# A hybrid encoder layer on one core: the last refill moves into the first output block, the descending norm comes one lane step later, and the two lanes get other rates

## The chip, the core and the metric

The kernel runs on one core of one Trainium2 chip. The core has a matrix engine (TensorE, PE in the profile, with PEld for its weight loads), a vector engine (VectorE, DVE), an activation engine (ScalarE, ACT), a general engine (GpSimd, POOL) and a queue engine (SyncE, SP) that issues nearly all transfers here. Operands lie in SBUF, matrix products are gathered in banks of PSUM. The metric is the device time of one execution in microseconds.

## The reference

One layer of an encoder with three groups of heads side by side, in 32-bit floats: `x + W_out @ concat[SSD, windowed attention, memory attention](RMSNorm(x))`. The rows are 1024 of a sample and 256 of a prompt, the model width is 2048. Cut to what matters:

```python
hn = rms_norm(x, norm_g)
proj = hn @ w_in
xbc, z_ssd, dt_raw, q, k, v, z_att, mq, z_mem = split_cols(proj, IN_SIZES)
xbc = jax.nn.silu(centred_dwconv(xbc, conv_w, conv_b))
...
y_f = ssd_scan(xs, dt[:, :, 0], A[0], Bm, Cm)
y_b = ssd_scan(xs[:, ::-1], dt[:, ::-1, 1], A[1], Bm[:, ::-1], Cm[:, ::-1])[:, ::-1]
y = (y_f + y_b + d_skip[:, None] * xs).reshape(b, T, SSD_WIDTH)
yg = (y * jax.nn.silu(z_ssd)).reshape(b, T, SSD_GROUPS, SSD_WIDTH // SSD_GROUPS)
o_ssd = rms_norm(yg, ssd_norm_g...)
o_att = window_attention(q, k, v, sink) * jax.nn.silu(z_att)
...
return x + jnp.concatenate([o_ssd, o_att, o_mem], axis=-1) @ w_out
```

`ssd_scan` is a chunked scan with chunks of 128 rows: within a chunk a masked product `C B^T` with decay, between chunks a state that is carried. It is run forwards and backwards over the rows. `ssd_norm_g` is a norm over each of two halves of 512 columns. The memory attention is a softmax attention of every row over 256 memory rows.

## The kernel before, in words

The 1280 rows are ten tiles of 128, in two groups of five. Tiles 0 to 7 are the sample, 8 and 9 the prompt. Group 0 is tiles 0 to 4, group 1 tiles 5 to 9.

**Blocks.** The program is a row of blocks, each a product of the rows of one group with 512 columns (token block, `block_tok`, L258 to L260) or with 256 columns transposed (feature block, `block_feat`, L293 to L295) over 16 places k of the 2048-deep sum. Every 32-bit product is made of three products of rounded parts: weights are split into `wh` and `wl` by `wsplit` (ACT L206, DVE L207), rows into `xH` and `xL`. A k of a token block is 15 products of 128x512, a pair of k's of a feature block 24 products of 128x320. The results gather in five PSUM banks (`acc`) and are taken out at the block's end (`zs`, `qs`, `yt`). Group 0 goes through most of its columns early, in another scheme. The part in question starts at about 540 us; its blocks in order are z1 (group 0), six x blocks, kv, q, za0, za1, z0, z1, mq, zm0, zm1, all of group 1, and then the output blocks o, four token blocks, of group 0's rows through W_out, before the output pair units from about 1575 us.

**Lanes.** All the rest (attention, scan, memory attention) is written as Python generators that hang in two lanes. Lane 0 has the attention (`attn`, `k_prep`), the memory attention (`mem_attn`); lane 1 has `dt_prep`, the ascending scan `ssd_up(t)` for t = 0 to 9 and the descending scan `ssd_down(t)` for t = 7 to 0, then 9 and 8. After each k of a block `pump(rates)` runs as many steps of each lane as `RATES` says: in a token block that number per k, in a feature block per pair of k's. A step is the code between two `yield`s. So where a lane's product stands between block products on PE is set by the rates and by the number of `yield`s; a scheduler then orders the instructions of each engine, moving loads forward. `need(fn, tiles)` runs a lane until the named tiles are done, whatever the rates say. PSUM for lane products is a ring of three banks, shared by all of them: a product waits till the one three before it has been taken out.

**The ascending tile** `ssd_up(t)`: C B^T into `pcb` (L823, L824), its copies `bth`, `btl`, `cb` (L827 to L830), a yield, then `cd`, `cbd`, `dco` on DVE (L833 to L839), and for each half the turned x, `pxs` (L858) with its copy `xs` on DVE (L860), then the decay rows `rf`, `rb` (L850, L922), `fh` and `fl` (L879, L887) and `pst` (L865) for the state.

**The descending tile** `ssd_down(t)`: loads of the part sums `yd`, the gate `zd`, the stored state `st`, and the turned diagonal part `ydT` (L1037); some yields; `norm_ssd`, which multiplies the tile before by its norm factor `yrs` (L998; the factor comes from ACT's sum of squares L1067 and three small POOL instructions, L123, L124, L1078); `diag_in(0)`, which turns `ydT` on PE into `pd` (L1043) and adds it (L1044); a yield; and per half the product with the state `pyb` (L1060), the gate, the sum of squares, a yield, and `turn_ssd(g)`, which turns the finished half of the tile before on PE (`pr`, L1007), copies it out (`so`, L1009) and stores it (`oT`, L1010). Only the tiles that start a descent (7 and 9) have nine yields at the start, the others three.

**The refill.** The output blocks read the rows from four quads of SBUF tiles, places k = 0 to 3, 4 to 7, 8 to 11, 12 to 15: quad 0 from the attention, quad 1 from the memory attention, quads 2 and 3 from the two halves of the scan. They are reloaded from DRAM by `fill_direct`: a load `chd` (L188) at one k, and a lag later a write of `xH` on ACT (L200 with gain, for the scan; L197 without) and of `xL` on DVE (L201, L198). `run` asks `after(q)` at k = 3, 7, 11, 15 of the block ahead, which first makes sure by `need` that the data are finished:

```python
            if after is not None and k % 4 == 3:
                pend.extend(after(k // 4))
```

For the scan that is `need(ssd_down, tiles 0 to 4)` at k = 11 of zm1, the last block ahead of the output blocks. At k = 9 of the third output block all that is left in the lanes is run; then come `seven_load` (L1105, L1106) and the sums for the output pair units, which read the finished rows of group 1.

Of the kernel before, what the change touches and what calls it, by code (L numbers as in the profile page):

```python
# [29 lines left out]
RBB = 4  # L30

RATES = ({'kv': (4.0, 1.0), 'z1': (2.2, 1.7)},
         {'kv': (1.4, 1.5), 'x': (2.1, 2.15), 'q': (2.2, 2.5), 'za': (2.05, 2.5), 'z0': (2.0, 2.6),
          'z1': (1.9, 2.65), 'mq': (1.9, 2.8), 'zm': (1.6, 2.85), 'o': (2.15, 2.25)})
FAR = 1e30

UNITS = (0, 8, 1, 9, 2, 10, 3, 11, 4, 12, 5, 13, 6, 7)
# [7 lines left out]
def hymba_encoder_kernel(  # L45
# [11 lines left out]
    def xrow(t):  # L57
        return x_sample[t * P:(t + 1) * P] if t < NS else x_prompt[(t - NS) * P:(t - NS + 1) * P]
# [24 lines left out]
    def psum(name):  # L83
        return mix.tile([P, 512], F32, tag="mix", name=name)
# [41 lines left out]
    def hv(ap, n=8):  # L126
        return ap.rearrange("p (h d) -> p h d", h=n)
# [50 lines left out]
    pend, loaded = deque(), deque()  # L178
# [31 lines left out]
    def w_laid(src, n):  # L210

        def load(k, raw):
            S.dma_start(raw, src[k])
        return load, n
# [12 lines left out]
    def w_out_rows(c):  # L227
        return w_laid(w_out_laid[c], 512)
# [173 lines left out]
    def ev_out(c0):  # L402
        def f(t, ps):

            if t in (0, 3):
                yt = rp.tile([P, 640], F32, tag="ch", name="yt", bufs=CH)[:, :512]
            else:
                yt = ev.tile([P, 512], F32, tag="evt" if t == 2 else "evu", name="yt")
            S.dma_start(yt, xrow(t)[:, c0:c0 + 512])
            V.tensor_add(yt, ps, yt)  # L410
            S.dma_start(y_first[t * P:(t + 1) * P, c0:c0 + 512], yt)
        return f
# [390 lines left out]
    def wb(name, dtype=F32, shape=(P, 512)):  # L803
        return mp.tile(list(shape), dtype, tag="wb", name=name, bufs=WBB)

    def ssd_up(t):
        first = t in (0, NS)
        last = t in (NS - 1, NT - 1)
        tok = slice(t * P, (t + 1) * P)
# [4 lines left out]
        for g in range(2):  # L814
            x = wb("xc", F32R, shape=(P, 4, P))
# [13 lines left out]
        cb = mp.tile([P, 2, P], F32, tag="cb", name="cb", bufs=1)  # L829
        A.activation(cb, hv(ps[:, :256], 2), AF.Copy)  # L830
        yield
        cd2 = wb("cd2", shape=(P, 2, P))
        V.tensor_mul(cd2, cb, ident.unsqueeze(1).broadcast_to([P, 2, P]))  # L833
        cbd = sm.tile([P, 2], F32, tag="s2", name="cbd", bufs=4)
# [2 lines left out]
        for g in range(2):  # L837
            c = slice(8 * g, 8 * g + 8)
# [31 lines left out]
        for g in range(2):  # L870
            c = slice(g * 512, (g + 1) * 512)
# [121 lines left out]
    def norm_ssd():  # L993

        if "y" in last_y:
            t, ys, rs = last_y.pop("y")
            for g in range(2):
                V.tensor_scalar(out=ys[g], in0=ys[g], scalar1=rs[:, g:g + 1], scalar2=None, op0=ALU.mult)  # L998
                last_y[g] = t, ys[g]
# [12 lines left out]
    def ssd_down(t):  # L1012
        first = t in (0, NS)
        last = t in (NS - 1, NT - 1)
        tok = slice(t * P, (t + 1) * P)
        ss = sm.tile([P, 2], F32, tag="s2", name="yss", bufs=4)
        if not last:
            cc = mp.tile([P, 2, P], F32, tag="btok", name="cc", bufs=1)
            S.dma_start(cc, xbc_d[10:12, :, tok].rearrange("f p c -> p f c"))
        ld = []  # L1020
        for g in range(2):
            c = slice(g * 512, (g + 1) * 512)

            y = mp.tile([P, 512], F32, tag="ya" if t % 2 else "rf", name="yd", bufs=2)
            S.dma_start(y, yp_d[t][:, c])
            if g == 0 and t < 5:
                z = mp.tile([P, 512], F32R, tag="xs", name="zd", bufs=2)
                S.dma_start(hv(z.bitcast(F32), 4), yT_d[:, :, tok])
            else:
                z = mp.tile([P, 512], F32, tag="xs", name="zd", bufs=2)  # L1030
                S.dma_start(z, z_d[g][t])
            st = None
            if not first:
                st = state[:, c] if last else wb("st2")
                S.dma_start(st, sb_d[t][:, c])
            d = mp.tile([P, 4, P], F32R, tag="rb", name="ydT", bufs=RBB)
            S.dma_start(d.bitcast(F32), yd_d[t][:, 4 * g:4 * g + 4, :])  # L1037
            ld.append((y, z, st, d))

        def diag_in(g):  # L1040
            ps = psum("pd")
            for j in range(4):
                T.transpose(ps[:, j * P:(j + 1) * P].bitcast(F32R), ld[g][3][:, j, :], identr)  # L1043
            V.tensor_add(ld[g][0], ld[g][0], ps)  # L1044

        for _ in range(9 if last else 3):
            yield
        norm_ssd()
        diag_in(0)
        yield  # L1050
        for g in range(2):
            c = slice(g * 512, (g + 1) * 512)
            y, z, st, _ = ld[g]
            if g == 0 and t < 5:
                zr, z = z, psum("pz")
                for j in range(4):
                    T.transpose(z[:, j * P:(j + 1) * P].bitcast(F32R), zr[:, j * P:(j + 1) * P], identr)
            if not last:
                pf = psum("pyb")
                T.matmul(pf, cc[:, g, :], state[:, c], start=True, stop=True)  # L1060
                y2 = wb("y3")
                V.tensor_mul(hv(y2), hv(pf), hb(eacs_all[:, t, 16 + 8 * g:24 + 8 * g], 8, 64))
                V.tensor_add(y, y, y2)
            V.tensor_mul(y, y, z)
            if g == 0 and t < 5:
                z = wb("zq")
            A.activation(z, y, AF.Square, scale=0.5, accum_out=ss[:, g:g + 1])  # L1067
            if not first and not last:
                V.tensor_mul(hv(state[:, c]), hv(state[:, c]), hb(cd_all[:, t, 16 + 8 * g:24 + 8 * g], 8, 64))
                V.tensor_add(state[:, c], state[:, c], st)  # L1070
            yield
            turn_ssd(g)
            if g == 0:
                diag_in(1)
                yield
        rs = sm.tile([P, 2], F32, tag="s2", name="yrs", bufs=4)
        rsqrt(rs, ss, 1.0 / 512, 2)
        G.tensor_scalar(out=rs, in0=rs, scalar1=0.5, scalar2=None, op0=ALU.mult)  # L1078
        last_y["y"] = t, [x[0] for x in ld], rs
        yield  # L1080
        if first:
            for _ in range(3):
                yield
            norm_ssd()
            yield
            yield
            for g in range(2):
                turn_ssd(g)
                yield
# [307 lines left out]
    def run(gen, rates, after=None, hold=0, lag=2, extra=None):  # L1397

        for k in gen:
            if after is not None and k % 4 == 3:  # L1400
                pend.extend(after(k // 4))
            if hold:
                for _ in range(2 if k < KT - 4 else 0):
                    if pend:
                        u = pend.popleft()()
                        next(u)
                        next(u)
            else:

                if loaded and (len(loaded) == lag or not pend or k >= KT - 4):  # L1410
                    next(loaded.popleft())
                if pend and k < KT - 4:
                    loaded.append(pend.popleft()())
                    next(loaded[-1])

            if k >= hold:
                pump(rates)
            if extra is not None:
                extra(k)
# [16 lines left out]
        yield  # L1436

    def refill_x(grp):
        def f(q):
            need(x_rows, [grp])  # L1440
            return [part(fill_direct, q, j, x_turned[grp, (4 * q + j) * P:(4 * q + j + 1) * P, :],
                         gain=vec[:, R_G + 4 * q + j:R_G + 4 * q + j + 1], norm=True) for j in range(4)]
        return f

    def refill_o(grp):
        def f(q):
            need((attn, mem_attn, ssd_down, ssd_down)[q], range(grp * 5, grp * 5 + 5))
            return [part(fill_direct, q, j, oT_d[q][grp][:, j, :],
                         gain=None if q < 2 else vec[:, R_SG + 4 * (q - 2) + j:R_SG + 4 * (q - 2) + j + 1])
                    for j in range(4)]  # L1450
        return f
# [63 lines left out]
    def tok(name, w, evac, after=None, grp=0):  # L1515
        run(block_tok(w, 5, evac), RATES[grp][name], after)
# [83 lines left out]
    def gate(name, c, after=None):  # L1600
        for b in range(2):
            feat(name, b, ev_gateT(c, 1, 2 * b), 1, after if b else None)
# [13 lines left out]
    queue(1, ssd_up, range(8, 10))  # L1616
    queue(1, ssd_down, range(9, 7, -1))
    tok("mq", w_in_rows("mq"), ev_raw(mq_d, 5), grp=1)
    gate("zm", 1, refill_o(0))
    queue(0, mem_attn, range(5, 8))  # L1620
    queue(0, mem_swap, [0])
    queue(0, mem_values, [1])
    queue(0, mem_attn, range(8, 10))
    for c in range(2):
        tok("o", w_out_rows(c), ev_out(c * 512), grp=1)
    for c in range(2, 4):
        j0 = 16 * (c - 3)
        for k in block_tok(w_out_rows(c), 5, ev_out(c * 512), before_last=lambda _: beside_step(j0 + 14)):
# [91 lines left out]
```

## Time and profile before

| what | value |
|---|---|
| median of 3 runs | 1795.46 us (1795.38 to 1795.53) |
| profiled execution | 1795.31 us, its span 1793.6 us |
| PE busy | 1777.4 us, 99% of the span, 10838 products |
| DVE, ACT, POOL busy | 1249.9, 919.5, 545.7 us (70%, 51%, 30%) |
| PE's granted clock | 1.00 throughout |
| 560 to 1345 us | PE busy for 775.1 of 785 us |

PE is nearly always busy, and so what it waits for is read from PE's own idle times: a row of the waits names the instruction that came late and what released it, with the total, the number and the longest. A row of the timeline gives start, duration, engine, line, operation, what it writes and reads, and in square brackets the idle time of that engine just before it and the releaser. In the chain of waits a row gives start, duration and what. The rows of the windows give start:end, length, the busy time of PE, PEld, DVE, ACT and POOL (with counts), then the clock, the share of the DMA engines and GB/s.

### The profile page before, as it was taken

What the parts mean: (1) busy time and instruction counts of PE and PEld (TensorE: products, weight loads), DVE (VectorE), ACT (ScalarE), POOL (GpSimd) and SP (SyncE); (2) the same over time, 40 slices, a digit from 0 to 9 for tenths busy, and PEclk for the clock granted to TensorE, in tenths of its full rate; (3) what the DMA queues carried; (4) which work ended last, traced back from release to release, by engine and by line L of the source; (5) the groups of instructions that cost most, each with busy time, mean ns of one, the idle gap of its engine ahead of it and who ended that gap; (6) DMA issues with size and microseconds to landing.
All of it is one profiled execution on the core that took longest, in us unless ns stands there. A gap on an engine that the chain in (4) does not pass through costs nothing. (4 is left out here: it accounts for less than half of the span.)

```text
span 1793.6 us, 31444 instructions
## 1 busy us (share of the span) xinstructions
PE 1777.4 (99%) x10838; PEld 1606.1 (90%) x10838; DVE 1249.9 (70%) x2358; ACT 919.5 (51%) x2049; POOL 545.7 (30%) x900
## 2 busy tenths in 40 slices
PE   9999999999999999999999999999999999999999
PEld 7789999999998989999889977777888888889999
DVE  5595788888768877877665566567775644766665
ACT  6554455554334765756465565544465533433332
POOL 0105889999710100001001000000100000058775
PEclk9999999999999999999999999999999999999999
DMA  8664455445446644343635645557876755644442
GB/s 300 191 179 123 136 153 151 137 149 154 126 152 199 191 141 148 120 161 115 188 111 178 190 147 165 175 154 258 257 225 202 231 181 164 205 145 147 146 142 78
DMA packets 208208, 301.12 MB, mean 168 GB/s; under 512 B 19569, under 2 KB 86193, under 8 KB 208049
## 3 DMA queue, kind: packets, MB, share of 16 engines
q1 hardware_dynamic: 207904, 299.06, 54.4%
q8 instruction: 85, 1.39, 0.3%
q14 instruction: 75, 0.61, 0.1%
q10 hardware_dynamic: 144, 0.06, 0.0%
HBM read 236.36 MB, written 62.69 MB: 167 GB/s over the span
## 5 line engine op out<-in xcount | busy, mean ns | idle before, releaser
L207 DVE TENSOR_TENSOR wl<-wraw,wh 128x512 fp32r<-128x512 f32 (+1 forms) x480 | 347.1, 725 | 232.3 <-ACT wh L206 224.0
L206 ACT ACTIVATE wh<-wraw 128x512 fp32r<-128x512 f32 (+1 forms) x480 | 292.5, 614 | 316.1 <-PE acc L260 154.3
L258 PE MATMUL acc<-wh,xH 128*128 128x512 f32 (+1 forms) x1088 | 419.4, 386 | 0.5 <-DVE v_all L337 0.4
L259 PE MATMUL acc<-wl,xH 128*128 128x512 f32 (+1 forms) x1088 | 410.7, 378 | 0.3 <-DVE wl L207 0.2
L260 PE MATMUL acc<-wh,xL 128*128 128x512 f32 (+1 forms) x1088 | 410.4, 377 | 0.0
L258 PEld LDWEIGHTS acc<-wh,xH 128*128 128x128 f32 x1088 | 204.6, 188 | 38.6 <-issue 3.8
L259 PEld LDWEIGHTS acc<-wl,xH 128*128 128x128 f32 x1088 | 204.8, 188 | 38.4 <-DVE wl L207 2.7
L260 PEld LDWEIGHTS acc<-wh,xL 128*128 128x128 f32 x1088 | 204.4, 188 | 36.8 <-issue 0.2
L293 PE MATMUL acc<-xH,wh 128*128 128x320 f32 x640 | 202.6, 317 | 0.0
L206 ACT ACTIVATE sh<-ws 128x384 fp32r<-128x384 f32 x176 | 91.4, 523 | 214.8 <-POOL ws L1205 123.0
L294 PE MATMUL acc<-xL,wh 128*128 128x320 f32 x640 | 198.9, 311 | 0.0
L295 PE MATMUL acc<-xH,wl 128*128 128x320 f32 x640 | 198.5, 310 | 0.0
L207 DVE TENSOR_TENSOR sl<-ws,sh 128x384 fp32r<-128x384 f32 x176 | 123.9, 707 | 103.4 <-ACT sh L206 100.4
L1205 POOL TENSOR_TENSOR ws<-wraw 128x128 f32<-128x128 f32 x176 | 111.1, 631 | 209.8 <-DMA wraw<-in_w_in_pairs_dram 78.5
L635 POOL COPY lg<-nsink 128x2 f32<-128x2 f32 x40 | 16.0, 399 | 390.4 <-PE ppt L663 239.9
L293 PEld LDWEIGHTS acc<-xH,wh 128*128 128x128 f32 x640 | 120.2, 188 | 3.3 <-issue 2.6
L294 PEld LDWEIGHTS acc<-xL,wh 128*128 128x128 f32 x640 | 120.3, 188 | 1.7 <-issue 1.4
L295 PEld LDWEIGHTS acc<-xH,wl 128*128 128x128 f32 x640 | 120.2, 188 | 0.8 <-issue 0.7
L1205 POOL TENSOR_TENSOR ws<-wraw,ws 128x128 f32<-128x128 f32 x176 | 116.5, 662 | 13.8
L1205 POOL TENSOR_TENSOR wraw<-wraw 128x128 f32<-128x128 f32 x176 | 113.4, 644 | 13.7
L1205 POOL TENSOR_TENSOR ws<-ws,wraw 128x128 f32<-128x128 f32 x176 | 117.1, 666 | 0.0
L362 DVE SCALAR_TENSOR_TENSOR c<-u,vec,c 128x638 f32<-128x638 f32 (+1 forms) x96 | 89.9, 939 | 11.6 <-ACT c L357 11.3
(437 smaller groups left out, 3941.9 us busy)
## 6 DMA issues: line engine op xcount, KB each, us to landing
wraw<-in_w_in_laid_dram SPq DMA_DIRECT2D x176, 256.0 KB, 2.9
wraw<-in_w_in_pairs_dram SPq DMA_DIRECT2D x112, 256.0 KB, 2.8
wraw<-in_w_out_laid_dram SPq DMA_DIRECT2D x64, 256.0 KB, 3.2
wraw<-in_w_out_pairs_dram SPq DMA_DIRECT2D x64, 256.0 KB, 2.8
rf<-ac SPq DMA_DIRECT2D x40, 256.0 KB, 3.8
rb<-ac SPq DMA_DIRECT2D x40, 256.0 KB, 5.0
wraw<-in_w_mem_laid_dram SPq DMA_DIRECT2D x32, 256.0 KB, 4.4
xst<-in_x_sample_dram SPq DMA_DIRECT2D x20, 256.0 KB, 4.5
```

The source lines that it names most:

```text
L206: a = A.activation(h, raw, AF.Copy)
L207: b = V.tensor_sub(l, raw, h.bitcast(F32))
L258: T.matmul(ps[t][:, :n], sh, h[:, :n], start=(k_ == 0), stop=False)
L259: T.matmul(ps[t][:, :n], sh, l[:, :n], start=False, stop=False)
L260: T.matmul(ps[t][:, :n], sl, h[:, :n], start=False, stop=(k_ == KT - 1))
L293: T.matmul(o, sh, cur["H", q][:, m, c], start=(k == 0), stop=False)
L294: T.matmul(o, sh, cur["L", q][:, m, c], start=False, stop=False)
L295: T.matmul(o, sl, cur["H", q][:, m, c], start=False, stop=(k == KT - 1))
L362: V.scalar_tensor_tensor(out=c[0], in0=u[:, k:k + n], scalar=cw[k], in1=c[0], op0=ALU.mult, op1=ALU.add)
L635: G.tensor_copy(lg[:, :, nk:nk + 1], ns8[:, rr, :].unsqueeze(2))
L1205: G.tensor_tensor(out=o, in0=x, in1=y, op=op)
```

## The change

Four edits. The count of PE's instructions is the same.

1. The refill. `run` now gives every k to `after`; `refill_o` has a table `when` that says at which k which quad is asked for. The attention and memory quads are asked for at k = 3 and 7 of zm1 as before, the two scan quads at k = 1 and 5 of the first output block in place of k = 11 and 15 of zm1. `need(ssd_down, ...)` moves with them. `refill_x` keeps its places by `divmod`.
2. The descending tile has four yields in place of three at its start, so the norm of the tile before and `diag_in(0)` come one lane step later (for all tiles but 7 and 9).
3. The ascending tiles 0 and 1 have one more yield, between `cb` and `cd`.
4. The rates of group 1's blocks from za on: from z0 to zm1 lane 0 gets more and lane 1 less, in the output blocks the other way round.

```diff
-         {'kv': (1.4, 1.5), 'x': (2.1, 2.15), 'q': (2.2, 2.5), 'za': (2.05, 2.5), 'z0': (2.0, 2.6),
-          'z1': (1.9, 2.65), 'mq': (1.9, 2.8), 'zm': (1.6, 2.85), 'o': (2.15, 2.25)})
+         {'kv': (1.4, 1.5), 'x': (2.1, 2.15), 'q': (2.2, 2.5), 'za': (2.1, 2.5), 'z0': (2.1, 2.5),
+          'z1': (2.05, 2.55), 'mq': (1.95, 2.7), 'zm': (1.75, 2.75), 'o': (2.1, 2.4)})
...
         A.activation(cb, hv(ps[:, :256], 2), AF.Copy)
         yield
+        if t < 2:
+            yield
         cd2 = wb("cd2", shape=(P, 2, P))
...
-        for _ in range(9 if last else 3):
+        for _ in range(9 if last else 4):
             yield
         norm_ssd()
         diag_in(0)
...
-            if after is not None and k % 4 == 3:
-                pend.extend(after(k // 4))
+            if after is not None:
+                pend.extend(after(k))
...
     def refill_x(grp):
-        def f(q):
+        def f(k):
+            q, last = divmod(k, 4)
+            if last != 3:
+                return []
             need(x_rows, [grp])
...
-    def refill_o(grp):
-        def f(q):
+    def refill_o(grp, when):
+        def f(k):
+            if k not in when:
+                return []
+            q = when[k]
             need((attn, mem_attn, ssd_down, ssd_down)[q], range(grp * 5, grp * 5 + 5))
...
-    gate("zm", 1, refill_o(0))
+    gate("zm", 1, refill_o(0, {3: 0, 7: 1}))
...
-        tok("o", w_out_rows(c), ev_out(c * 512), grp=1)
+        tok("o", w_out_rows(c), ev_out(c * 512), None if c else refill_o(0, {1: 2, 5: 3}), grp=1)
```

The lines of `ssd_up` behind the new yield, and of all that follows, have a number two higher afterwards.

Three places in the order of instructions. First PE in block z1 of group 0, at the turned x of the ascending tile 0 (`pxs`, both halves); before:

```order
L260 MATMUL acc<-wh,xL_877 128x512
L258 MATMUL acc<-wh,xH_876 128x512
L259 MATMUL acc<-wl,xH_876 128x512
L260 MATMUL acc<-wh,xL_877 128x512
L858 MATMUL pxs<-identr,xc 128x128 x8
L258 MATMUL acc<-wh,xH_876 128x512
L259 MATMUL acc<-wl,xH_876 128x512
L260 MATMUL acc<-wh,xL_877 128x512
```

Afterwards, at the first half and, 15 block products later, at the second:

```order
L258 MATMUL acc<-wh,xH_876 128x512
L259 MATMUL acc<-wl,xH_876 128x512
L260 MATMUL acc<-wh,xL_877 128x512
L860 MATMUL pxs<-identr,xc 128x128 x4
L258 MATMUL acc<-wh,xH_876 128x512
```

```order
L258 MATMUL acc<-wh,xH_876 128x512
L259 MATMUL acc<-wl,xH_876 128x512
L260 MATMUL acc<-wh,xL_877 128x512
L860 MATMUL pxs<-identr,xc 128x128 x4
L258 MATMUL acc<-wh,xH_1190 128x512
```

The two halves stood next to each other and now have one k of block products between them.

Second DVE at a descending tile in zm0, from the weight split ahead of the norm to the diagonal part's sum (`yd<-yd,pd`, which follows `pd` on PE); before:

```order
L207 TENSOR_TENSOR wl<-wraw,wh 128x512
L998 TENSOR_SCALAR yd<-yd,yrs 128x512 x2
L649 RECIPROCAL den<-den 128x2
L651 TENSOR_SCALAR lg<-lg,den 128x256 x2
L643 ISA lg,nm<-pdist,psc,nsink 128x256
L643 ISA nm 128x1
L643 ISA lg,nm<-pdist,psc,nsink 128x256
L643 ISA nm 128x1
L1044 TENSOR_TENSOR yd<-yd,pd 128x512
```

and afterwards at the tile at the same count from the start of the descent:

```order
L1066 TENSOR_TENSOR yd<-yd,zd 128x512
L207 TENSOR_TENSOR wl<-wraw,wh 128x512
L676 TENSOR_TENSOR oT<-po,za 128x256
L604 TENSOR_REDUCE qss<-sq 128x8
L1000 TENSOR_SCALAR yd<-yd,yrs 128x512 x2
L611 TENSOR_TENSOR q<-q,qr 128x512
L207 TENSOR_TENSOR wl<-wraw,wh 128x512
L618 TENSOR_TENSOR qh<-q,qh 128x4x64 x2
L1046 TENSOR_TENSOR yd<-yd,pd 128x512
```

Before, the norm stood in front of the softmax rows of one attention pair; now it comes after the output of one attention tile and in front of the query norm of another, since the lanes stand otherwise to each other.

Third SP at the refill of the scan quads, the stores of the last scan tile (`oT<-so`), the loads (`chd`), weights (`wraw`) and decay rows (`rf`, `rb`); before:

```order
L1010 DMA oT_0_160<-so 512x1x128
L213 DMA wraw<-in_w_out_laid_dram 128x512
L850 DMA rf<-ac_194 128x512
L1010 DMA oT_0_158<-so 512x1x128
L1010 DMA oT_0_160<-so 512x1x128
L850 DMA rb<-ac_194 128x512
L850 DMA rf<-ac_194 128x512
L188 DMA chd<-oT_0_158 128x640 x2
L320 DMA zT_1_121<-zs 128x640
L188 DMA chd<-oT_0_158 128x640
L850 DMA rb<-ac_194 128x512
L188 DMA chd<-oT_0_158 128x640
```

and afterwards:

```order
L1012 DMA oT_0_158<-so 512x1x128
L1012 DMA oT_0_160<-so 512x1x128
L852 DMA rb<-ac_194 128x512
L852 DMA rf<-ac_194 128x512
L188 DMA chd<-oT_0_158 128x640 x4
L852 DMA rb<-ac_194 128x512 x2
L213 DMA wraw<-in_w_out_laid_dram 128x512 x2
L852 DMA rb<-ac_194 128x512
L188 DMA chd<-oT_0_160 128x640
L213 DMA wraw<-in_w_out_laid_dram 128x512
L812 DMA bc<-xbc_d 128x4x128
L188 DMA chd<-oT_0_160 128x640 x2
```

Before, the four loads of the first scan quad (158) are mixed with a store of the last gate rows of zm1 (`zT`) and a load of decay rows, so they stand at that block's end; now they stand in a row inside the first output block, with two loads of decay rows and two of weights queued right behind them.

## The prediction

> **What bounds the kernel now.** I read the page's head first, then the busy time of the stretch in which the changed rows stand, then PE's waits there, and last the rows around each long wait.
>
> ```profile
> span 1793.6 us, 31444 instructions
> PE 1777.4 (99%) x10838; PEld 1606.1 (90%) x10838; DVE 1249.9 (70%) x2358; ACT 919.5 (51%) x2049; POOL 545.7 (30%) x900
> ...
> 560.00:1345.00 785.00, 775.12 (x4853) 679.28 (x4852) 552.30 (x1208) 450.86 (x1123) 67.76 (x124) 1.00 0.56 173
> ```
>
> TensorE is busy for 1777.4 of 1793.6 us, and the last columns of the third row have its granted clock at 1.00. Only 16.2 us are not PE work, and 785 − 775.1 = 9.9 of them lie between 560 and 1345 us, where the moved rows are. The change neither adds nor removes a product, so the busy time stays: only the idle time can move, and a gain of more than 16 us is excluded. PE's waits of that stretch, in total, number and longest:
>
> ```profile
> PE pcb L823 <- ACT pT L664: 2.7, 1, 2.7
> PE pd L1043 <- DMA ydT<-yd: 2.7, 2, 2.4
> PE pxs L858 <- DVE xs L860: 1.5, 1, 1.5
> PE pxs L858 <- ACT kL L510: 1.2, 1, 1.2
> PE pmt L767 <- ACT wh L206: 0.8, 1, 0.8
> PE ppt L663 <- DVE nm L643: 0.5, 1, 0.5
> PE pst L865 <- DVE ya L883: 0.2, 1, 0.2
> ```
>
> Five waits of the first four rows make 2.7 + 2.7 + 1.5 + 1.2 = 8.1 us. Each stands at an operation that one of the edits shifts. I take them one by one.
>
> **Refill of the scan quarters.** The last chain of the group 0 scan, and what follows, by the chain of waits (first three rows) and the timeline:
>
> ```profile
> 1319.94 0.62 ACT so L1009 x2
> 1320.56 3.77 DMA oT<-so
> 1324.40 5.69 DMA chd<-oT
> ...
> 1329.48 0.47 PE L258 MATMUL acc<-wh,xH 128*128 128x512 f32 x1
> ...
> 1330.11 0.83 ACT L200 ACTIVATE xH<-chd,vec 128x640 fp32r<-128x640 f32 x1 [3.17 <-DMA chd<-oT]
> ...
> 1332.72 0.65 ACT L664 ACTIVATE pT<-ppt 128x256 f32<-128x256 f32 x2
> ...
> 1333.15 0.49 PE L823 MATMUL pcb<-bc 128*128 128x128 f32 x2 [2.73 <-ACT pT L664]
> ...
> 1336.38 1.56 ACT L200 ACTIVATE xH<-chd,vec 128x640 fp32r<-128x640 f32 x2
> ...
> 1338.86 0.64 ACT L879 ACTIVATE fh<-xf 128x512 fp32r<-128x512 f32 x1
> ```
>
> The store takes 3.77 us and the reload 5.69, so the first fill can run 10.2 us after the copy out of PSUM began. ACT reaches that fill too early and sits 3.17 us; pT, which would free a PSUM bank of the ring of three, stands behind it; PE waits 2.73 for the bank. That is the only mechanism here: what stands between the fill and pT are copies and one more fill.
>
> After the change the fills are emitted at k = 3 of the first output block, and the memory attention's mpT and the scan's fh stand behind them on ACT. The forced end of the scan, which is now three lane steps at once, issues its two turns back to back. I call their start T. By the rows above the copies are done at T + 1.2, the stores at T + 5, the first reload at T + 10.7. ACT then has four fills (1.56 a pair), and by the order a weight copy, one mpT and two decay rows among them, which I put at 0.6 each and 0.6 for the pair, and fh (0.64): T + 10.7 + 3.1 + 1.8 + 0.6 = T + 16.2 for its end. The order has 45 block products and 48 small ones between the turns and the first product with fh. The small ones are of 128x128 or 128x256.
>
> ```profile
> 564.71 0.39 PE L258 MATMUL acc<-wh,xH 128*128 128x512 f32 x1
> 564.94 0.39 PE L259 MATMUL acc<-wl,xH 128*128 128x512 f32 x1
> ...
> 1319.30 1.04 PE L1007 MATMUL pr<-identr,yd 128*128 128x128 f32 x8
> ```
>
> Starts of block products are 0.23 us apart, and 8 turns take 1.04, so PE gets there at about T + 45 × 0.23 + 48 × 0.13 = T + 16.6. Those times are nearly equal, and DVE's difference fl comes some 0.7 after fh, so this place is a coin toss. I put 0.8 us there. At the end of the block before, a turn now also waits for a bank behind two zs rows, wh and so, which I put at 0.4. Net: −2.7 + 0.8 + 0.4 = −1.5. Ends: −2.7 (neither wait) and +2.0 (the 2.73 stands there again, with one wait of 1.2 and one of 0.8 from the table beside it). The first fill is written at k = 3 and read at k = 8, five k's of at least 15 × 0.23 = 3.45 us later; that does not bind. On SP's queue the reloads wait for the stores' landing, and two loads of decay rows and two weight loads stand behind all four: held by up to 3.8 us, which I count as zero, since these weights are for later k's; uncovered it would be those 3.8.
>
> [...]
>
> **One more lane step ahead of the descending norm.** The reload of the transposed diagonal part sets pd:
>
> ```profile
> 1242.31 0.39 PE L293 MATMUL acc<-xH,wh 128*128 128x320 f32 x1
> ...
> 1250.74 0.51 PE L1043 MATMUL pd<-identr,ydT 128*128 128x128 f32 x4 [2.42 <-DMA ydT<-yd]
> ...
> 1299.90 0.51 PE L1043 MATMUL pd<-identr,ydT 128*128 128x128 f32 x4 [0.31 <-DMA ydT<-yd]
> ...
> DMA to landing us min/median/max: 3.8/4.6/5.5
> ```
>
> PE came 2.42 and 0.31 us too early, at two of the eight tiles concerned. Both are in the two zm blocks, which run from 1242.31 to the output blocks' first product at 1329.48: 87.2 us for 16 pairs of k's, 5.45 us a pair, and with 2.85 steps of lane 1 to a pair 1.9 us a step. Alone the step would leave 0.5 of the 2.42, but the rates also move the place, and counting the order's products with the durations above, PE has 10.9 us between the last pyb of the tile before and this pd where it had 6.2. So both waits go. One other place loses distance (11.5 to 8.8 us by the same count), for which I leave 0.2. Net −2.5; ends −2.7 and 0 (the wait comes up at another tile).
>
> The same step gives DVE time for the norm's factor from POOL:
>
> ```profile
> DVE yd L998 <- POOL yrs L1078: 13.4, 8, 2.2
> ...
> 1246.63 0.19 POOL L123 TENSOR_SCALAR yrs<-yss 128x2 f32<-128x2 f32 x1 [0.80 <-ACT zd L1067]
> 1246.91 0.73 POOL L124 TENSOR_TENSOR yrs<-yrs,mhalf 128x2 f32<-128x2 f32 x1
> 1247.72 0.22 POOL L1078 TENSOR_SCALAR yrs<-yrs 128x2 f32<-128x2 f32 x1
> ...
> 1211.26 0.41 POOL L123 TENSOR_SCALAR yrs<-yss 128x2 f32<-128x2 f32 x1 [8.60 <-ACT zd L1067]
> ```
>
> DVE waits 13.4 us in eight tiles. None of it shows as a PE wait in the table but through what queues behind it, so I count it as zero. The chain on POOL is 0.19 + 0.73 + 0.22 plus hand-overs, some 1.3 us, less than a step. [...]
>
> What is paid: everything that follows in the tile comes a step later too. At the third tile from the end of the scan, the order puts the attention's ppt right behind two DVE products of the scan, for which PE has 3.1 us of work and DVE needs 3.8: +0.7, taken as +0.6 since the products overlap a little. Ends: 0, and the rival below.
>
> **The second yield in the first two ascending tiles.**
>
> ```profile
> 568.09 0.88 DVE L194 SCALAR_TENSOR_TENSOR chd<-chd,vec,rbc 128x640 f32<-128x640 f32 x1 [3.66 <-DMA chd<-in_x_turned_dram]
> ...
> 571.31 0.41 DVE L509 CAST kT<-pk 128x256 fp32r<-128x256 f32 x1
> ...
> 571.76 0.38 ACT L510 ACTIVATE kL<-pk 128x256 fp32r<-128x256 f32 x1 [4.79 <-DVE kT L509]
> ...
> 572.20 0.53 PE L858 MATMUL pxs<-identr,xc 128*128 128x128 f32 x4 [1.24 <-ACT kL L510]
> ...
> 634.93 0.17 DVE L391 COPY u<-carry 128x4 f32<-128x4 f32 x1 [1.84 <-DMA xbc_d<-u]
> ...
> 638.21 0.69 DVE L860 COPY xs<-pxs 128x512 f32<-128x512 f32 x1
> ...
> 638.96 0.53 PE L858 MATMUL pxs<-identr,xc 128*128 128x128 f32 x4 [1.47 <-DVE xs L860]
> ```
>
> Tile 0: the second pxs needs a bank that kL frees at 572.14; by the order it now has 15 products, 3.4 us, in front of it. The 1.24 us go: −1.2 (ends −1.2 and 0).
> Tile 1: DVE is held until 634.93 by a store, with or without the edit, and the copy that frees the bank comes 3.3 us behind (638.21) since eight rows stand between. The order keeps those rows ahead of the copy and now lets an attention product (psc) ask for the bank. I put 0 (ends −1.5 and +1.0, one more copy row and a half).
>
> **Rates.** They add nothing; they decide where each lane operation falls between block products. The waits I have not named, 0.8 + 0.5 + 0.2 = 1.5, will be drawn anew; I take 1.5 again, net 0. Ends −1.5 and +5.4 (four new waits of the 1.35 mean of the first four rows' shorter ones, 1.2 and 1.5). In the last output blocks the scan's last tile now ends one to two k's later, ahead of these rows:
>
> ```profile
> 1510.08 0.33 SPq L1106 DMA_DIRECT2D rb__17755<-oT  x1
> ...
> 1514.49 0.82 ACT L1110 ACTIVATE rb__17755<-rb__17755,vec 128x640 f32<-128x640 f32 x1
> ```
>
> The sums that use them are queued with nothing for PE until the pair units some 60 us on; counted as zero, price under the fourth rival.
>
> **Sum.** −1.5 − 2.5 + 0.6 − 1.2 + 0 + 0 = −4.6 us. The profiled execution took 1795.31 us, the median 1795.46; the difference of 0.15 is within what the runs vary, and I put the sum on the median: 1790.9.
>
> **Rivals.**
> First, all five waits go and nothing new comes: −8.1, 1787.4. For it: each stands at an operation that moves away. Against it: the fill chain and PE arrive together at the output block, by the sum above.
> Second, the waits only move: a program that fills 99% with PE has few free places, and store, reload and PSUM ring stay as they are. 1794 to 1796.
> Third, the reload is quicker in the new place: at the 3.8 us of the shortest landing of ydT in place of 5.69 the fills run 1.9 us sooner and the 0.8 does not appear, 1790.1. Against it: SP issues four at once. [...]
> Fourth, the late end of the scan: if the two k's (6.8 us) by which the last store moves come through to the sums ahead of the pair units, 1790.9 + 6.8 = 1797.7. Against it: those 60 us.
> Fifth, and slower: with everything in the tile one step later, each of the eight descending tiles asks for a PSUM bank while DVE still works through the products of the tile, as pxs did at 638.96. The price is that row's 1.47 each, 11.8 for eight, against a gain of 5.2 without the 0.6: 1795.46 − 5.2 + 11.8 = 1802.1. It decides for slower from six tiles on (6 × 1.47 − 5.2 = 3.6). For it: DVE is busy 552 of 785 us and bursts at each tile. Against it: only one tile did so before, and that an ascending one.
> Sixth, the change doesn't move anything. The order excludes that for pxs, pd and fills; what could happen is that the time does not answer, 1795.5.
>
> **Numbers.** 0.2% is 3.6 us, about what a measurement of this kernel can tell from no change. Chances: forecast 0.46 (1789 to 1793), all gone 0.12, waits move 0.22, quick reload 0.03, late end 0.05, slower 0.10, no answer 0.02. Below 1791.87 lie three quarters of the forecast's (0.35), 0.12, 0.03 and 0.03 of the second: faster 0.53. Slower: 0.10 and 0.02 of the others, 0.12. Same 0.35. The range, 1787.2 to 1797.0, leaves out the slower rival and the late end, 0.15.
>
> **What would show it.** No wait of 2.7 at pcb in the last block ahead of the output blocks, and xH after chd with no ACT idle time over 1 us there; a wait at pst or pmo in the first output block of about 0.8. No wait of pd for ydT over 0.3; DVE's wait for yrs well under 13.4. No wait at 572; one at 639 on psc instead of pxs. The forecast is wrong if PE's idle time between 560 and 1345 is above 8 us, or if a new wait of over 1 us comes in blocks za0 to zm1, which I can only see as an order and not as times.

## The result, and the profile after

The changed kernel takes 1792.89 us in the median of 18 runs (1789.91 to 1796.83), the kernel before 1795.62 us beside it (18 runs, 1789.89 to 1799.27). The ratio is 0.9981 with a 95% interval of 0.9974 to 0.9989: 3.4 us faster, between 2.0 and 4.7 (the two medians alone differ by 2.7). The three runs known before the change agreed within 0.15 us; over more runs both kernels spread by 7 to 9 us, and part of what follows is why. On another chip the same two gave 0.9976 (0.9968 to 0.9985). Two runs of the kernel before, of 3539.69 and 4505.99 us, lie far outside all others and count in no ratio.

The head of the profile page and the windows row of 560 to 1345 us, of the changed kernel:

```profile
span 1791.0 us, 31429 instructions
...
PE 1777.5 (99%) x10838; PEld 1605.0 (90%) x10838; DVE 1248.7 (70%) x2358; ACT 922.2 (51%) x2049; POOL 549.6 (31%) x900
...
560.00:1345.00 785.00, 779.82 (x4882) 683.75 (x4881) 549.89 (x1208) 445.27 (x1107) 71.96 (x124) 1.00 0.56 171
```

PE's work is the same to 0.1 us and the span is 2.6 us shorter. In the stretch of the moved rows PE is idle for 785 − 779.8 = 5.2 us where it was 9.9. PE's waits there:

```profile
PE pyb L1062 <- ACT so L1011: 1.1, 1, 1.1
PE pmt L767 <- DVE mpr L759: 1.1, 1, 1.1
PE psc L641 <- DVE nm L643: 0.9, 1, 0.9
PE acc L293 <- DVE zs L309: 0.5, 1, 0.5
PE psc L641 <- ACT pT L664: 0.5, 1, 0.5
PE pd L1045 <- DVE nm L643: 0.3, 1, 0.3
PE psc L641 <- ACT qT L625: 0.2, 1, 0.2
```

None of the five waits of before is left, and no wait is over 1.2 us where three were over 1.4. What stands there now are smaller ones at other places; the two longest are a `pmt` of 1.09 at 853.86 us and a `pyb` of 1.13 at 1247.91 us, which is in zm0. (`psc` is the attention's product of keys and queries, `pmt` turns the memory attention's rows `mpr` on PE.) From 1345 to 1600 us it went the other way. There the kernel before had one wait of 0.2; after, the same view has

```profile
PE pmt L767 <- DVE mpr L759: 0.9, 2, 0.8
PE pst L868 <- DVE fl L889: 0.2, 1, 0.2
```

and PE's idle time grew from 0.2 to 1.4 us. The rest of the difference, 0.9 us, lies in the first 540 us, where the two programs are the same and one execution differs from the next by as much (2.5 us idle before, 3.3 in this profile, 2.4 in another profile of the changed kernel, e8 below).

The refill as it now runs, by the timeline: the turns of the last scan tile on PE, the copies on ACT, the stores and reloads as SP issues them, and the fills.

```profile
1335.86 1.04 PE L1009 MATMUL pr<-identr,yd 128*128 128x128 f32 x8
...
1336.65 1.07 ACT L1011 ACTIVATE so<-pr 128x512 f32<-128x512 f32 x2
...
1337.25 1.21 SPq L1012 DMA_DIRECT2D oT<-so  x2
...
1341.54 1.74 SPq L188 DMA_DIRECT2D chd<-oT  x4
...
1346.32 1.67 ACT L200 ACTIVATE xH<-chd,vec 128x640 fp32r<-128x640 f32 x2 [0.51 <-DMA chd<-oT]
...
1348.88 1.54 ACT L200 ACTIVATE xH<-chd,vec 128x640 fp32r<-128x640 f32 x2
```

From the turns to the first fill it is 10.5 us, and ACT waits 0.51 us for the reload where it waited 3.17. By the same timeline fh ends 15.7 us after the turns, the first product with fh comes at 16.1 without a wait, and the next, with fl, at 16.8 after a wait of 0.2 us. The store took 4.28 us and the reload 4.75, together 9.0, where the rows before had 3.77 and 5.69, together 9.5.

### The profile page after: what moved, and what is told of

Read it like the earlier page. It is cut to its first block, busy times and chain, and to the rows that moved or that the text cites. A ratio compares the mean times of both kernels' runs of the same rounds, so it can differ in the third digit from the quotient of the medians.

```text
span 1791.0 us, 31429 instructions
## 1 busy us (share of the span) xinstructions
PE 1777.5 (99%) x10838; PEld 1605.0 (90%) x10838; DVE 1248.7 (70%) x2358; ACT 922.2 (51%) x2049; POOL 549.6 (31%) x900
## 4 chain that ended last, share of the span: by engine, by line
PE 71%; issue 7%; POOL 7%; DVE 6%; DMA 6%; ACT 3%; SPq 0%; POOLq 0%; ACTq 0%; DVEq 0%
PE acc L258 8%; PE acc L260 8%; PE acc L259 8%; PE acc L293 5%; PE acc L1237 5%; PE acc L295 5%; PE acc L294 5%; PE acc L1235 5%; PE acc L1236 5%; POOL ws L1207 4%; PE accm L1236 2%; PE accm L1235 2%; PE accm L1237 2%; POOL wraw L1207 2%; PE po L673 1%
```

## The experiments

Four kernels with one edit alone ran together on one chip (e1 to e4), four more on another (e5 to e8), the last four on a third (e9 to e12). "Idle" is PE's idle time from 560 to 1600 us in the profiled execution, from the windows as above. "Clock" is the number of runs whose mean granted clock was recorded under 1.000. The kernel before ran beside each call. Where a profile has a stretch at half clock (e1 to e5), the longer products there count as busy (in e5 a block product of 128x512 took 0.63 us at 1340.65 where it took 0.39 at 1336.66), so their idle time tells a little too little. A ratio is taken against the runs of the kernel before on the same chip; two ratios from different chips compare less well.

| kernel | ratio (95%) | idle, us | clock |
|---|---|---|---|
| before | 1 | 10.1 | 61 of 91 |
| the change | 0.9981 (0.9974 to 0.9989) | 6.6 | 1 of 18 |
| e1, refill only | 1.0007 (0.9998 to 1.0016) | 9.3 | 8 of 11 |
| e2, step only | 1.0029 (1.0018 to 1.0041) | 12.4 | 9 of 11 |
| e3, rates only | 1.0008 (0.9998 to 1.0017) | 11.3 | 7 of 11 |
| e4, yield only | 0.9981 (0.9972 to 0.9990) | 7.1 | 8 of 11 |
| e5, all but refill | 0.9996 (0.9985 to 1.0007) | 8.9 | 11 of 12 |
| e6, all but step | 0.9976 (0.9965 to 0.9986) | 6.0 | 2 of 12 |
| e7, all but rates | 0.9995 (0.9985 to 1.0005) | 9.7 | 5 of 12 |
| e8, the change again | 0.9976 (0.9968 to 0.9985) | 7.1 | 1 of 12 |
| e9, all but yield | 0.9988 (0.9976 to 1.0000) | 8.4 | 4 of 12 |
| e10, yield and rates | 0.9990 (0.9978 to 1.0002) | 8.7 | 5 of 12 |

### One edit alone

**e1.** Only the refill moves.

```diff
-    gate("zm", 1, refill_o(0))
+    gate("zm", 1, refill_o(0, {3: 0, 7: 1}))
...
+        tok("o", w_out_rows(c), ev_out(c * 512), None if c else refill_o(0, {1: 2, 5: 3}), grp=1)
```

> Of the four edits only the refill: the scan quads are asked for at k = 1 and 5 of the first output block. Theory A (each edit removes the wait at its own place and adds little elsewhere): the 2.7 us at pcb near 1333 us go, the waits at 572, 639 and 1251 us stay, PE's idle time from 560 to 1345 us falls from 9.9 to 7.2 us, ratio to the kernel before 0.9985. Rival B (the waits are drawn anew whenever the lanes are shifted): another wait of 1 to 3 us comes in zm1 or in the first output block, the idle time stays at 9 to 11 us, ratio 0.9995 to 1.0005.

It gained nothing, and the idle time to 1345 us is 8.4 us. The timeline of e1 at the end of zm1:

```profile
1332.43 0.83 ACT L200 ACTIVATE xH<-chd,vec 128x640 fp32r<-128x640 f32 x1 [2.38 <-DMA chd<-oT]
1333.17 0.42 ACT L318 ACTIVATE zs<-acc 128x320 f32<-128x320 f32 x1
...
1335.04 0.66 ACT L664 ACTIVATE pT<-ppt 128x256 f32<-128x256 f32 x2
...
1335.48 1.11 PE L663 MATMUL ppt<-identr,lg 128*128 128x128 f32 x4 [1.94 <-ACT pT L664]
```

It is the picture of before, 1.94 for 2.73 us. The fill is asked for in the next block, but with the old rates the scan is done early, and the scheduler puts loads and fill in front of that block's last copies (zs), where ACT waits for the reload as it did: the last copy `so` begins at 1325.56 us here, in zm1, and at 1336.65 in the changed kernel, in the first output block. So the place in the program alone doesn't move the fill; the data must be late too.

**e2.** Only the fourth yield of the descending tile.

```diff
-        for _ in range(9 if last else 3):
+        for _ in range(9 if last else 4):
```

> Of the four edits only the fourth yield of the descending tile. Theory A: the waits of pd for ydT (2.7 us) go, those at 572, 639 and 1333 us stay, idle time from 560 to 1345 us 7.2 us, ratio 0.9985. Rival B: pd no longer waits for ydT, but a later row of the descending tile (pyb, ppt, pr) waits instead for 1 to 3 us, idle time 9 to 11 us, ratio 0.9995 to 1.0005.

This one is slower, by more than the change gains. The timeline of e2:

```profile
1291.50 0.51 PE L1043 MATMUL pd<-identr,ydT 128*128 128x128 f32 x4 [2.26 <-DMA ydT<-yd]
...
1333.70 0.40 ACT L922 ACTIVATE rf<-rf,wj_all 128x128 f32<-128x128 f32 x1 [2.96 <-DMA rf<-ac]
...
1335.01 0.49 PE L858 MATMUL pxs<-identr,xc 128*128 128x128 f32 x2 [2.70 <-ACT pT L664]
```

The pd wait is not gone, it came up at a later tile with nearly the old length. The scan ends later, the refill stays where it was, and now ACT waits 2.96 us for a load of decay rows; PE waits 2.70 behind it. SP issued that load at 1327.79 us, right behind the two stores of the scan's end, and it landed 5.9 us later; the median of the loads of `rf` is 4.2 there. That the stores slow it is likely and not shown.

**e3.** Only the rates, as in the change's first diff lines.

> Of the four edits only the rates. Theory A: rates take away no cause, so pcb near 1333 us and the pd waits stay in some size; idle time from 560 to 1345 us 9 to 10 us, ratio 0.9995 to 1.0005. Rival B: the rates alone redraw as much as the rest together; the idle time moves by more than 2 us either way, ratio under 0.9988 or over 1.0012.

Neither faster nor slower, but not by leaving things alone: the waits of pcb and of pd for ydT are gone, and waits of 1.6 and 0.9 us at pst, of 1.7 at pmt near 1358 us and of 1.5 at pmt near 885 us have taken their place.

**e4.** Only the second yield in the ascending tiles 0 and 1.

```diff
         yield
+        if t < 2:
+            yield
         cd2 = wb("cd2", shape=(P, 2, P))
```

> Of the four edits only the second yield in the ascending tiles 0 and 1. Theory A: the 1.24 us at 572 us go, the wait at 639 us stays as one on psc of 1 to 1.5 us, the waits from 1240 us on stay; idle time from 560 to 1345 us 8.6 us, ratio 0.9993. Rival B: the one or two lane steps by which all later work of lane 1 is late redraw the waits from 640 to 1345 us, idle time there changes by more than 1.5 us either way.

The largest gain of one edit. PE's waits from 560 to 1345 us in e4:

```profile
PE pcb L823 <- ACT pT L664: 2.2, 1, 2.2
PE pd L1045 <- DMA ydT<-yd: 2.0, 1, 2.0
PE pmt L767 <- DVE mpr L759: 0.9, 1, 0.9
PE psc L641 <- ACT pT L664: 0.5, 1, 0.5
PE pr L1009 <- ACT pT L664: 0.4, 1, 0.4
```

Both waits of pxs are gone, at 572 and at 639 us, 2.7 us of the 3.0 by which the idle time is less; a psc near 647 us waits 0.49. The waits of pd (2.00 at 1248 us) and pcb (2.19 at 1330 us) stay.

The kernels without this edit have the same rows up to there, and their profiles show how much the two waits vary: at 572 us 1.24, 1.35, 0, 0.30 and 0.91 us (before, e1, e2, e3, e9), at 639 us 1.47, 1.63, 0.90, 1.67 and 0.81. The profiled execution of before had more than the mean of both (0.8 and 1.3 us).

### One edit left out

**e5.** The change with the scan quads asked for at k = 11 and 15 of zm1.

```diff
-    gate("zm", 1, refill_o(0, {3: 0, 7: 1}))
+    gate("zm", 1, refill_o(0, {3: 0, 7: 1, 11: 2, 15: 3}))
...
-        tok("o", w_out_rows(c), ev_out(c * 512), None if c else refill_o(0, {1: 2, 5: 3}), grp=1)
+        tok("o", w_out_rows(c), ev_out(c * 512), None, grp=1)
```

> The changed kernel with the scan quads asked for at k = 11 and 15 of zm1 as before. Theory A: the wait at the end of zm1 (pcb or another product, behind a fill that waits for its reload on ACT) is back with 2 to 3 us; idle time from 560 to 1345 us 7.5 to 8 us where the changed kernel has 5.2; ratio to the kernel before 0.9993. Rival B: no wait over 1 us comes back there, idle time 5 to 6 us, ratio as for the whole change.

The wait is back, in the first output block; the timeline of e5:

```profile
1337.28 0.40 ACT L924 ACTIVATE rb<-rb,wj_all 128x128 f32<-128x128 f32 x1 [2.51 <-DMA rb<-ac]
...
1340.06 0.79 PE L867 MATMUL pst<-fh,bth 128*128 128x512 f32 x1 [2.55 <-ACT fh L881]
```

As in e2, a load of decay rows issued right behind the two stores holds ACT. It lands 5.1 us after its issue, and the median of the loads of `rb` is 4.9 there: it isn't slow, it is issued late. With e1 this says what the refill edit is worth: nothing by itself, some 2 to 3 us once the scan ends later (0.9996 against 0.9976 on the same chip, with intervals that just touch).

**e6.** The change with three yields in the descending tile.

```diff
-        for _ in range(9 if last else 4):
+        for _ in range(9 if last else 3):
```

> The changed kernel with three yields in the descending tile as before. Theory A: pd waits for ydT again, 1 to 3 us in total, idle time from 560 to 1345 us 6.5 to 8 us, ratio 0.999. Rival B: with the new rates pd finds its data landed even so, no pd wait over 0.5 us, idle time about 5 us.

As fast as the whole change, and pd doesn't wait for ydT: the place of pd is moved far enough by the rest. The pyb near 1247 us doesn't wait either. The price of leaving it out is a wait of 1.30 at pst, and 14.5 us in which DVE waits for POOL's factor where the change has 12.7; neither shows in the time.

**e7.** The change with the old rates.

> The changed kernel with the old rates. Theory A: the waits at 572, 1251 and 1333 us stay away without the rates; idle time from 560 to 1345 us within 1.5 us of the changed kernel's 5.2, ratio as for the whole change, and the new waits of 1.2 us for mpr in the first two output blocks, which I take to come from the output blocks' rates, are gone. Rival B: idle time 7 us or more, ratio 0.9995 or above.

Most of the gain is gone, by the point values (0.9995 for 0.9976, with intervals that just touch), and the idle time to 1345 us is 6.9 us, between what the theory and the rival say. pd waits 2.36 us for ydT near 1290 us, pyb 1.84 near 1314, and a turn (pr) 1.13 near 1516 us, among the last of the scan, which ends later with fewer steps per k. The waits for mpr in the output blocks are not gone (0.96 near 1354 us), so the rates of those blocks are not what makes them.

**e8.** The change again, on the chip of e5 to e7.

> The changed kernel again, on the same chip as the three with one edit undone. Idle time from 560 to 1345 us 5.2 us and from 1340 to 1600 us 1.4 us in each execution if the waits are fixed by the order; if they differ by more than 1 us from the first profile, the waits also hang on how long transfers take from run to run. Ratio 0.9974 to 0.9989.

The waits stand at the same places as in the first profile, but their sizes differ by up to 0.9 us (a psc of 0.88 at 1073 us is absent here, pyb near 1245 us waits 1.49 for 1.13), and three of 0.3 to 0.5 us are new (640, 1368 and 1422 us). The stretch to 1345 us has 4.5 us, that from 1345 to 1600 us 2.6 for 1.4. So the sizes also hang on something that differs from run to run.

**e9.** The change without the yield in tiles 0 and 1.

```diff
-        if t < 2:
-            yield
```

> The changed kernel without the second yield in the ascending tiles 0 and 1. Theory: that yield carries more than half of the gain, so without it the waits of pxs at 572 and 639 us are back (1.2 and 1.5 us), the granted clock is under 1.00 in half or more of the runs, ratio to the kernel before 0.9990 to 1.0000. Rival (the edits add up without touching each other): the wait at 572 us alone comes back, the clock stays at 1.00 in most runs, ratio 0.9983.

0.9988 lies between the two, and the interval holds both. The waits of pxs are back with 0.9 and 0.8 us; the clock is under 1.000 in 4 of 12 runs, not in half.

**e10.** The yield and the rates, with the old refill and the old step.

```diff
-        for _ in range(9 if last else 4):
+        for _ in range(9 if last else 3):
...
-    gate("zm", 1, refill_o(0, {3: 0, 7: 1}))
+    gate("zm", 1, refill_o(0, {3: 0, 7: 1, 11: 2, 15: 3}))
...
-        tok("o", w_out_rows(c), ev_out(c * 512), None if c else refill_o(0, {1: 2, 5: 3}), grp=1)
+        tok("o", w_out_rows(c), ev_out(c * 512), None, grp=1)
```

> The yield and the rates, without the fourth yield of the descending tile and with the old refill. Theory (the later refill only takes back what the later norm costs): as good as the whole change, no wait over 1.6 us, idle time from 560 to 1600 us 6 to 7 us, ratio 0.9972 to 0.9982. Rival (single results multiply, 0.9981 x 1.0008): ratio 0.9985 to 0.9995, with the waits of the rates alone near 1340 to 1358 us (1.6 and 1.7 us) still there.

The theory looks wrong, and isn't excluded: the idle time is 8.7 us where it had 6 to 7, and the ratio of 0.9990 lies in the rival's range, but its interval reaches into the theory's range. Against e6, which differs from this by the refill alone, e10 is slower on its point value (0.9990 for 0.9976), with 2.0 us of waits at pst behind fh and 1.2 at pmt, as with the rates alone; the two ran on different chips and their intervals overlap.

### The clock

In several of these profiles (e1 to e5) the granted clock fell to 0.50 for a few us in the midst of the work. Those of before and after show it only behind PE's last product, at the end of the span (the last 1.0 us of before, 0.4 of after). The trace lists each change of the clock: the low stretches of e1 to e5 last 3.413 us each, and begin a whole number of 3.413 us after the first change (in e4 388 of them after its 5.1 us). In before and after the stretch listed at full clock is 1785.17 us long, 523 times 3.4133. So I read two profiles by that grid. PE's busy time and the granted clock (the column after the count) in e4, around its wait at 1329.72, and in the kernel before, around its wait of 2.73 at 1333.15:

```profile
1322.63:1326.05 3.42, 3.42 (x26) 1.00 0.93 260
1326.05:1329.46 3.41, 1.48 (x9) 1.00 0.93 359
1329.46:1332.87 3.41, 3.15 (x13) 0.50 0.92 266
1332.87:1336.29 3.42, 3.42 (x23) 1.00 0.99 239
```

```profile
1324.94:1328.36 3.42, 3.42 (x26) 1.00 0.83 191
1328.36:1331.77 3.41, 2.06 (x15) 1.00 1.01 398
1331.77:1335.18 3.41, 2.03 (x16) 1.00 0.77 236
1335.18:1338.60 3.42, 3.42 (x23) 1.00 0.97 239
```

The wait in e4 is the shorter one, 2.19 us, but 1.94 of it fell into one window, which was busy for 1.48 of 3.41 us; the next window ran at half clock, which at half of 3.4 us is an estimated 1.7 us of lost work. The longer wait of before was parted by the grid, each of its two windows was busy for 2.0 us or more, and the clock stayed at 1.00. To see which waits are followed by half clock, two kernels hold PE at 34 places, with a short product `p` and sums on DVE that the next weights `h` wait for:

```diff
+        p = psum("hold")
+        T.matmul(p, identr, cur["H", 0][:, 0, :512], start=True, stop=True)
+        while w > 0:
+            n = min(w, 512)
+            V.reduce_sum(out=r, in_=p[:, :n], axis=AX.X)
+            w -= n
+        V.tensor_scalar(out=r, in0=r, scalar1=0.0, scalar2=None, op0=ALU.mult)
+        V.tensor_scalar(out=h, in0=h.bitcast(F32), scalar1=r, scalar2=None, op0=ALU.add)
```

> The changed kernel with about 34 holds put into its blocks from the x blocks on: at two places of each block the weights of the next k are held back on DVE by a chain of sums over one PSUM bank, 200 to 3600 elements long, so that PE waits for 0.5 to 5 us. Only a zero is added to the weights. Theory: waits under 1.5 us never lower the granted clock; those from 1.6 us on do so in a share that grows with their length, and then the clock is 0.50 for 3.4 us, which costs 1.7 us more. Rival (the clock falls only after a wait of over 3.4 us): no window under 1.00 after any wait shorter than that.

> The same with other lengths in another order, 900 to 2600 elements, so that most waits are between 1 and 3.5 us. Theory: between 1.6 and 3.4 us some waits lower the clock and some of the same length do not. Rival: none below 3.4 us does.

They take 1946.82 and 1940.57 us, in one run each. Counting the windows of the grid at full clock, up to PE's last product, by PE's busy share, and how many were followed by half clock:

| busy share of the window | e11 and e12 | all other profiles |
|---|---|---|
| under 0.49 | 31 of 31 | 4 of 4 |
| 0.49 to 0.66 | 7 of 19 | 2 of 19 |
| over 0.66 | 0 of 1016 | 0 of 6216 |

Both theories fell in part. The rival did: a wait need not be 3.4 us long (e4's was 2.19). Mine had the wrong quantity: waits under 1.5 us were followed by half clock too, where two or three fell into one window (0.78, 0.69 and 0.52 us in e12's window from 1412.7 us). In these counts the fall goes with the idle sum in a window of 3.413 us: it came after all 35 windows of the first row, which were busy for 0 to 0.48 of their length, and after none of the 7232 of the last. Between, it isn't sharp: the lowest share without a fall is 0.49 and the highest with one 0.65. How long the clock stays low isn't explained: one window in e1 to e5, but two or three in 20 of the 38 low stretches of e11 and e12.

## Why the prediction was right or wrong

The range held and the direction was right; the forecast of −4.6 us was larger than the −3.4 (2.0 to 4.7) of the first comparison and close to the −4.3 of e8's ratio. 0.9981 is just inside the 0.2% that I had set as the limit of no change; that the kernel is faster at all rests on the interval. Of the signs of being wrong that I had named, the idle time (5.2 us, limit 8) did not come, but the other did: a new wait of over 1 us in blocks za0 to zm1, the pyb of 1.13 us in zm0.

**The stretch from 560 to 1345 us: right in its sum, not in its terms.** I had 9.9 − 4.6 = 5.3 us of idle time left there; it has 5.2. The five waits of 8.1 us went, and on balance 3.4 us came back; I had put 3.5 (1.2 at the refill, 0.2 at pd, 0.6 for the crowding, and 1.5 that stay at tile 1). That the two figures agree is in part luck: of the 2.7 us set for the refill and tile 1 none came to 1345 us in the first profile, and pyb (1.1 us, 0.6 set for the crowding) and the waits not named (3.2 us, 1.5 set) made up for it. Beyond 1345 us the sum ended, and there 1.2 us came on top.

**Refill.** The chain came as worked out (first fill 10.5 us after the turns, for 10.7), and the product with fl waits 0.2 us where I put 0.8. What failed is "after the change the fills are emitted at k = 3 of the first output block" as a cause by itself: e1 asks for them there and kept 1.94 us of the wait. In the changed kernel they stay there because the scan ends 11 us later, by the other edits.

**The descending step.** "So both waits go" held, but the step was not the reason: e6 leaves it out and pd doesn't wait for ydT, e2 has it alone and pd waits 2.26 at another tile. The distance came from the other edits. That DVE's wait for POOL would be well under 13.4 us was wrong: it became 12.7 (e2, with the step alone, has 11.5). The crowding that I put at ppt (0.6) didn't come there; in its place pyb waits behind the copy so near 1247 us for 1.1 to 1.5 us. It does so in all profiles that have the step and the new rates (after, e8, e5, e9), and not without the step (e6) or with the old rates (e7). So the step, together with the new rates, brings this wait. In e6 a pst waits 1.30 us instead, and the times don't differ.

**The yield.** Tile 0 went as forecast, though its 1.2 us rest on one execution (0 to 1.35 in five). At tile 1 I expected the wait to stay as one on psc, for 0 net; 0 to 0.45 us of it are left in the two profiles of the changed kernel, so the term was too small by more than 1 us. By e4 this is the largest single gain.

**Rates.** Here is the term that made the sum too large: "net 0" over the waits not named, with the output blocks not looked at. PE's idle time from 1345 to 1600 us grew by 1.2 us in the first profile, by 2.4 in e8. To 1345 us they were larger too: pmt, psc and acc make 3.2 us where I had 1.5. The late end of the scan cost nothing in the changed kernel; e7 shows that it can (1.13 near 1516 us).

**Rivals.** "The waits only move" describes each edit alone rather well (e1 and e3), and the whole not. The slower rival, a PSUM bank asked for while others hold it, came true only for the step alone (1.0029), by one wait behind ACT and one behind a transfer, not at all eight tiles. The quicker reload came by half (4.75 us, where 5.69 and 3.8 were set against each other), but the store took 0.5 longer, and ACT still waits 0.51 for it.

**Not foreseen: the clock.** I took a wait's price as its length. Of the 91 runs of the kernel before that were recorded beside the experiments, 61 had a mean clock under 1.000; of the changed kernel's 30, 2. The mean clock of those runs was about 0.9991 and 0.9999, and 0.0008 × 1795 is an estimated 1.4 us of the gain. The runs bear out the price: on e8's chip the medians of the kernel before are 1794.55, 1796.25, 1797.68 and 1799.43 us at recorded clocks of 1.000, 0.999, 0.998 and 0.997 (10, 15, 7 and 3 runs), some 1.6 us a step; the other two chips are rougher. One window at half clock lowers the mean by an estimated 0.001 (1.7 of 1793.6 us). Between runs at 1.000 on that chip alone the medians are 1794.55 (10 runs) and 1791.97 (11): 2.6 us, as much as between the two profiles, which both ran at full clock. So a third to two fifths of the gain are the clock by this estimate, and that the measured 3.4 us come near the forecast is to that extent luck. The likely reason is that waits over 1.4 us gave way to smaller ones that don't fill half a window; in the profiles of before and after themselves neither set of waits lowered it (the least busy windows have shares of 0.55 and 0.68). And a gain is possible without it: e4 has 0.9981 with 8 of its 11 runs under 1.000.

What stays open: why the load of decay rows took so long in e2 (no run took the stores ahead of it away), what makes the waits for mpr, and how much each edit is worth within the whole, since the intervals of e5 and e7 just touch that of e8 and e9 and e10 ran on another chip.

## What to carry to other kernels

In this program, 99% full of products, edits that shift work between them didn't add: the four alone multiply to 1.0025, together they gave 0.9976 to 0.9981, so cost and test them together and then leave each one out: left out of the four, the step made no difference in the time (e6). Here a load asked for later in the program moved only when its data were late too. And of two schedules with the same idle time, the one with short waits that stand far apart looks better: in these profiles each of the 35 windows of 3.413 us in which PE was busy for under 0.49 was followed by half clock, which cost an estimated 1.7 us more for each window at it.

## What the runs showed of the hardware

Up to PE's last product, the granted clock fell to 0.50 for one window of 3.413 us at a time in e1 to e5 and for one to three in e11 and e12, on the grid counted from the execution's first change of the clock. It did so after 35 of 35 windows in which PE was busy for under 0.49, 9 of 38 from 0.49 to 0.66, none of 7232 above. The first change comes 7.4 us after the start of before's profile, 5.4 after that of the changed kernel's and 5.1 after that of e4, so the same wait can fall on the grid otherwise from run to run: before's 2.73 us at 1333.15 were parted by it and the clock stayed at 1.00, e4's 2.19 at 1329.72 had 1.94 in one window and cost an estimated 1.7 us more. That is likely a part of why runs of one kernel spread over several us: of the 91 runs of the kernel before, 61 had a mean clock under 1.000 and 30 did not, and on e8's chip their medians go from 1794.55 us at 1.000 to 1799.43 at 0.997.
